# Twelve weight loads of 1 MB each issued as four loads of 256 KB

## The chip, the cores and the metric

The kernel runs on one core of a Trainium2 chip. The metric is the device time of one execution in microseconds (us), as the median of the runs shown. The core has five engines that run beside one another: TensorE (PE, matrix products; its weight loads are listed apart as PEld), VectorE (DVE), ScalarE (ACT), GpSimd (POOL) and SyncE (SP). Each has a queue of instructions of its own and works through it in order. Transfers are issued by SP, ACT or POOL and carried out by the core's 16 DMA engines.

## The reference

One layer of a bidirectional encoder over 1024 tokens (a grid of 16 rows by 64 columns) of width 1024. One projection feeds two groups of heads:

```python
h = _rmsnorm(x, norm_gain[l])
proj = h @ w_in[l]
q_a, k_a, v_a, g_a, q_b, k_b, v_b, g_b = jnp.split(proj, split_at, axis=-1)
...
o_a = _gqa_blocked(q_a, k_a, v_a) * jax.nn.silu(g_a)
o_b = _neighbourhood_attn(q_b..., k_b..., v_b..., na_rpb[l])
o_b = o_b * jax.nn.silu(g_b)
mixed = jnp.concatenate([o_a, o_b], axis=-1)
x = x + mixed @ w_out[l]
return _rmsnorm(x, final_norm_gain)
```

Group A is attention over all 1024 keys (8 query heads, 2 key heads of 64, normalised and rotated by row and column). Group B is attention over a window of 8 rows by 16 columns with a learned bias (8 heads of 64). Everything is float32. The input projection has 3328 columns, the output projection 1024.

## The kernel before

**Weights.** The two weight matrices are cut into 17 groups of 256 columns: `w[0]` to `w[12]` of the input projection and `wo[0]` to `wo[3]` of the output projection (groups 13 to 16). A group is 1024 x 256 float32, 1 MB, and lies in memory as 128 partitions of 8 KB each. It is loaded into a tile `raw` ([128, 8, 256]), of which there are two in turn, so that group g+2 takes the buffer of group g. From `raw` four steps make the operands of the products, a pair of float16 tiles (high and low part): `prep_a` (L281, sum of squares on ACT), `prep_b` (L293 to L295, the sum over partitions on PE, then a power on POOL that gives the scale), `prep_c` (L300, high part on ACT, two halves) and `prep_d` (L307, low part on DVE, two halves). After the last of these the buffer is free, and group g+2 is loaded into it: `load_w`, L159, one DMA issued by POOL. Groups 0 and 1 are loaded at the start by SP, the latter in four pieces of 256 KB (L187).

**Order.** The order of PE is written out by hand for the whole kernel, that of the others only for the opening (up to L875). After it a planner places the instructions of ACT, DVE, POOL and SP on their queues, going by the order in which the program lists them and by its own estimate of when each can run.

The order in which the program lists things comes from a small class, `Flow`. The work is a sequence of slots (`step`). One slot lists, in this order, what is due at "pre", the scores of one attention unit, what is due at "mid", the low part and the transpose of the unit before, what is due at "post", some chunks of the projections (`fill`), and the last products of an older unit. `at(delay, pos, fn)` puts `fn` into the slot that is `delay` slots further on, at the place `pos`. `sums_now` (L341) runs behind a projection chunk and lists `prep_b` of the group that is next, `prep_c` and `prep_d` one slot further on, and `load_w(g + 2)` two slots further on, at "pre" (L349).

**Stages.** In the opening the input is normalised and transposed and the first projections run. Stage A (about 105 to 360 us) has 64 units of the global attention, one head of 128 queries each: scores on PE (L592, L594), their extreme on DVE (L601), two exponentials on ACT (L603 in float16, L604 in float32), the difference of both on DVE (L609), and one DMA transpose of both parts, [128, 2048] float16, issued by SP (L614). Three such tiles are in turn, so ACT's L603 three units later writes where the transpose has read. Four units later PE multiplies the transposed weights by the values (L623 to L625). Between the units run the projections of groups 3 to 8. Stage B (about 360 to 565 us) has 64 units of the neighbourhood attention with smaller scores and transposes (L681 to L705), beside the projections of groups 9 to 12 (the gates) and the output projection; the rest is the output projection of the last rows and the final norm.

Twelve loads are touched by the change, those of groups 5 to 16. Going through the slots, group 5 is loaded at unit 0 of A, 6 at 6, 7 at 14, 8 at 26, 9 at 38, 10 at 50, 11 at 62, then 12 at unit 5 of B, 13 at 15, 14 at 25, 15 at 42 and 16 at 47. Their readers `prep_a` stand at units 10, 22, 34, 46, 58 of A and 2, 11, 21, 37, 43, 49, 54 of B.

Of the kernel before, what the change touches and what calls it, by code (L numbers as in the profile page):

```python
# [42 lines left out]
class Flow:  # L43
# [8 lines left out]
    def at(self, delay, pos, fn, *a):  # L52
        self.due.setdefault((self.slot + delay, pos), []).append((fn, a))
# [35 lines left out]
def kernel(ctx: ExitStack, tc: tile.TileContext, x: bass.AP, w: bass.AP, wo: bass.AP,  # L89
# [3 lines left out]
    act, dve, pool, pe, sp = nc.scalar, nc.vector, nc.gpsimd, nc.tensor, nc.sync  # L93
# [10 lines left out]
    at = fl.at  # L104
# [48 lines left out]
    raw, wp, late, x2 = {}, {}, {}, {}  # L153

    def load_w(g):
        raw[g] = wraw.tile([P, KC, GC], F32, tag="raw", name=f"raw{g}")
        if g in gate:
            pool.tensor_copy(raw[g][:, 0, :1], xr[gate[g]][:, 1:])
        pool.dma_start(raw[g], w[g] if g < 13 else wo[g - 13])  # L159

    xts, gate = [], {}
    ones = area(0, [P], F32)[:1]
# [178 lines left out]
    def sums_now():  # L341

        while pend:
            g = pend.pop(0)
            prep_b(g)
            at(1, "pre", prep_c, g)
            at(1, "post", prep_d, g)
            if g + 2 < 17:
                at(2, "pre", load_w, g + 2)  # L349
# [86 lines left out]
    def qa_gen(hh, up):  # L436
        def evac(pt):
            g = QA + hh
            stg = slot("stg1", [P, 2, 4, P], F16)
            a, b = (0, D) if hh == 0 else (D, 0)  # L440

            def fin(q):
                at(2, "pre", lambda: act.activation(stg[:, :, :, a:a + D], q, AF.Copy))
                at(2, "mid", lambda: dve.tensor_tensor(stg[:, :, :, b:b + D], q, stg[:, :, :, a:a + D], op=OP.subtract))

                def tr():
                    sp.dma_start_transpose(qTa[hh][:, 2 * up:2 * up + 2].rearrange("p i h t -> p (i h) t"),
                                           stg.rearrange("p i a b -> p (i a b)"))
                at(2, "post", tr)
            norm_rope(g, up, pt, 4, 0, fin)  # L450
        yield from proj_pair(QA + hh, up, from_h, evac)

    def kva_gen(up):
        def evac(pt):
            both = slot("stg1", [P, 8, P], F16)
            stg, stg_l = both[:, :6].rearrange("p (i a) b -> p i a b", a=3), both[:, 6:]
            vs = pt[:, :, P:].rearrange("p a (h d) -> p a h d", d=D)
            at(1, "pre", lambda: act.activation(va[:, 2 * up:2 * up + 2, :, 0, :], vs, AF.Copy, scale=2.0 ** -14))

            def vlo():  # L460
                for i in range(2):
                    dve.scalar_tensor_tensor(va[:, 2 * up + i, :, 1, :], vs[:, i], 2.0 ** -14,
                                             va[:, 2 * up + i, :, 0, :], op0=OP.mult, op1=OP.subtract)
            at(1, "mid", vlo)

            def fin(k):
                def hi():
                    act.activation(stg[:, :, :2, :D], k, AF.Copy)
                    act.activation(stg[:, :, :2, D:], k, AF.Copy)
                at(2, "pre", hi)  # L470

                def lo():
                    for h, to in ((0, stg[:, :, 2]), (1, stg_l)):
                        dve.tensor_tensor(to.rearrange("p i (e d) -> p i e d", d=D),
                                          k[:, :, h, None, :].to_broadcast([P, 2, 2, D]),
                                          stg[:, :, h].rearrange("p i (e d) -> p i e d", d=D), op=OP.subtract)
                at(2, "mid", lo)

                def tr():
                    sp.dma_start_transpose(kTa[:, 2 * up:2 * up + 2].rearrange("p i a t -> p (i a) t"),  # L480
                                           both[:, :6].rearrange("p a b -> p (a b)"))
                    sp.dma_start_transpose(klo1[:, 2 * up:2 * up + 2], stg_l.rearrange("p a b -> p (a b)"))
                at(2, "post", tr)
            norm_rope(KVA, up, pt[:, :, :P], 2, 1, fin)
        yield from proj_pair(KVA, up, from_h, evac)
# [92 lines left out]
    def group(g, gens):  # L578

        def first(gen):  # L580
            prep(g + 1)
            yield from gen
        return [first(gens[0]) if g < 16 else gens[0], *gens[1:]]
# [255 lines left out]
    k, q = [kva_gen(up) for up in UP], group(1, [qa_gen(0, up) for up in UP])  # L839
# [30 lines left out]
    x_rs(7)  # L870
    x_y(7)
    load_w(2)
    gate[3] = 5
    x_lo(7, dve)
    load_w(3)  # L875

    for p in range(11):
# [165 lines left out]
```

## Time and profile before

| | |
|---|---|
| runs | 611.54, 610.44, 607.44 us; median 610.44 us |
| the profiled execution | 611.81 us, of which the span in the trace is 610.0 us |
| granted clock of TensorE, mean | 0.967 |
| busy: PE, DVE, ACT, POOL | 88%, 72%, 65%, 20% of the span |
| transfers issued by POOL | 19.92 MB in 3312 packets, 11.6% of the DMA engines' time |
| transfers issued by SP | 75.66 MB in 242306 packets, 67.7% |
| the weight loads of L159 | 15, median time from issue to landing 6.7 us (groups of `w`), 5.9 us (`wo`) |

The loads of groups 5 to 16 are issued at 101.92, 129.72, 160.71, 205.59, 252.25, 303.04 and 348.76 us, and in stage B at 381.51, 408.73, 438.29, 485.97 and 505.71 us.

A row of a timeline gives the start, the duration, the engine, the line, the operation and its operands, and in brackets how long the engine stood idle before it and what ended that. A row of a group gives the least, median and largest duration in nanoseconds. For a DMA issue the duration is the time that the issuing queue needed, not the time of the transfer; that is "to landing". A busy share of DMA engines near 1 means that packets were in work on them all the time, whatever they moved.

### The profile page before, as it was taken

The page shows a single profiled execution, that of the slowest core. Times are in us where ns is not written, and L with a number is a line of the kernel's source. Part 1 is how long each engine was busy: PE and PEld are TensorE (multiplying, and loading weights), DVE is VectorE, ACT ScalarE, POOL GpSimd, SP SyncE. Part 2 cuts the span into 40 slices and gives each one's busy share as a digit, 9 for nine tenths or more (in the row PEclk, how much of TensorE's full clock was granted, in tenths as well). Part 3 has the DMA queues.
Part 4 walks back from the last instruction along what each step waited for, and adds up shares of the span by engine and source line. Part 5 has one row for each costly group of instructions (what it writes and reads, how often), then busy time and mean ns, then how long its engine had stood idle before and what let it go on. Part 6 is the DMA issues. An engine that isn't in the chain of part 4 may idle for free.

```text
span 610.0 us, 13863 instructions
## 1 busy us (share of the span) xinstructions
PE 534.4 (88%) x5541; PEld 405.4 (66%) x5541; DVE 440.6 (72%) x986; ACT 394.9 (65%) x647; POOL 119.3 (20%) x150
## 2 busy tenths in 40 slices
PE   3587989799988979979888979999999789889794
PEld 1376878577864535547666767877777567668684
DVE  4688676987977948957977847586877866778332
ACT  5552454878859858858667727677689986674210
POOL 2396788410000000000000000110111221112100
PEclk9978999999999979989899999999999898999899
DMA  8989433799999999999799894548486996687422
GB/s 231 225 160 247 96 105 106 136 213 195 204 198 168 197 173 169 206 207 187 155 183 210 155 217 122 118 76 134 103 149 122 172 212 145 134 140 183 95 62 70
DMA packets 245972, 97.26 MB, mean 159 GB/s; under 512 B 236561, under 2 KB 237201, under 8 KB 243986
## 3 DMA queue, kind: packets, MB, share of 16 engines
q1 hardware_dynamic: 242306, 75.66, 67.7%
q0 software_dynamic: 3312, 19.92, 11.6%
q10 hardware_dynamic: 288, 0.79, 0.5%
q8 instruction: 43, 0.70, 0.5%
q14 instruction: 23, 0.19, 0.1%
HBM read 31.33 MB, written 4.19 MB: 58 GB/s over the span
## 4 chain that ended last, share of the span: by engine, by line
PE 44%; DMA 14%; issue 14%; DVE 13%; POOL 6%; ACT 5%; SPq 1%; DVEq 0%; POOLq 0%; ACTq 0%
PE pj L369 14%; PE wt L369 7%; DMA ar<-p 6%; PE po L369 5%; PE kb L369 4%; DMA ar<-ar 4%; PE s L592 3%; PE s L594 2%; POOL nt L417 2%; PE sb L674 2%; DVE whl L307 2%; ACT p L604 2%; DVE p L601 1%; PE sb L673 1%; ACT p L603 1%
## 5 line engine op out<-in xcount | busy, mean ns | idle before, releaser
L369 PEld LDWEIGHTS <-hT 128*128 128x128 f16 x2112 | 205.6, 100 | 68.5 <-issue 15.4
L369 PE MATMUL pj<-whl,hT 128*128 128x256 f16 x1584 | 189.2, 275 | 3.4 <-DMA hT<-xhl 1.8
L601 DVE CUSTOM_DVE_ANT_0 p<-s,sm 128x1024 f32<-128x1024 f32 x64 | 82.0, 1281 | 15.4 <-PE s L594 13.9
L603 ACT ACTIVATE p<-s,nm,sm 128x1024 f16<-128x1024 f32 x43 | 51.8, 1204 | 51.1 <-DMA ar<-p 23.4
L369 PE MATMUL wt<-whl,hT 128*128 128x256 f16 x528 | 68.0, 286 | 14.9 <-ACT whl L300 7.1
L604 ACT ACTIVATE p<-s,nm,sm 128x1024 f32<-128x1024 f32 x64 | 76.8, 1200 | 0.0
L609 DVE TENSOR_TENSOR p<-p,p 128x1024 f16<-128x1024 f32 x43 | 52.8, 1229 | 21.7 <-ACT p L604 21.6
L369 PE MATMUL po<-whl,mA 128*128 128x256 f16 x384 | 65.8, 277 | 0.0
L684 ACT ACTIVATE rq<-ar,mx,sm 128x384 f32<-128x384 f32 (+1 forms) x64 | 43.0, 673 | 28.6 <-DVE mx L683 28.4
L295 POOL TENSOR_TENSOR sm<-wss,mh 128x1 f32<-128x1 f32 x17 | 11.0, 645 | 250.1 <-DVE wss L294 237.4
L369 PEld LDWEIGHTS <-mA 128*128 128x128 f16 x512 | 48.7, 100 | 12.3 <-issue 5.0
L369 PE MATMUL po<-whl,mB 128*128 128x256 f16 x192 | 53.1, 277 | 0.0
L592 PE MATMUL s<-kTa,rq 128*128 128x512 f16 x128 | 39.5, 391 | 14.6 <-ACT p L604 14.6
L623 PE MATMUL pv<-va,ar 128*128 128x64 f16 x384 | 39.3, 194 | 8.7 <-DMA ar<-p 7.4
L307 DVE SCALAR_TENSOR_TENSOR whl<-raw,sm,whl 128x1024 f16<-128x1024 f32 (+1 forms) x33 | 44.8, 1371 | 1.9 <-ACT whl L300 1.9
L685 ACT ACTIVATE ar<-ar,mx,sm 128x384 f16<-128x384 f32 (+1 forms) x64 | 42.9, 674 | 1.1
L623 PEld LDWEIGHTS <-ar 128*128 128x128 f16 x384 | 34.7, 99 | 13.1 <-DMA ar<-p 9.3
L300 ACT ACTIVATE whl<-raw,sm 128x1024 f16<-128x1024 f32 x34 | 37.1, 1138 | 5.0 <-POOL sm L295 4.9
L681 DVE CUSTOM_DVE_ANT_0 ar<-sb,bias 128x384 f32<-128x384 f32 x48 | 26.6, 555 | 18.4 <-PE sb L674 15.4
L625 PE MATMUL pv<-va,ar 128*128 128x64 f16 x384 | 39.3, 194 | 0.0
L624 PE MATMUL pv<-va,ar 128*128 128x64 f16 x384 | 39.3, 194 | 0.0
L690 DVE TENSOR_TENSOR ar<-rq,ar 128x384 f16<-128x384 f32 (+1 forms) x64 | 34.1, 533 | 4.8 <-ACT ar L685 4.8
(196 smaller groups left out, 1069.3 us busy)
## 6 DMA issues: line engine op xcount, KB each, us to landing
raw<-in_w_dram POOLq DMA_DIRECT2D x11, 1024.0 KB, 6.7
raw<-in_wo_dram POOLq DMA_DIRECT2D x4, 1024.0 KB, 5.9
x<-in_x_dram SPq DMA_DIRECT2D x7, 512.0 KB, 6.4
khh<-ar SPq DMA_DIRECT2D x16, 128.0 KB, 3.7
x2b<-in_x_dram POOLq DMA_DIRECT2D x4, 512.0 KB, 5.9
x<-in_x_dram POOLq DMA_DIRECT2D x4, 512.0 KB, 6.8
out_dram<-x2b SPq DMA_DIRECT2D x8, 256.0 KB, 3.0
out_dram<-x SPq DMA_DIRECT2D x7, 256.0 KB, 2.9
```

The costliest lines, as they stand in the source:

```text
L307: dve.scalar_tensor_tensor(wp[g][1][:, s], raw[g][:, s], col(S_ + g), wp[g][0][:, s], op0=OP.mult, op1=OP.subtract)
L369: pe.matmul(*o[0], **o[1])
L592: pe.matmul(s[:, c * 512:(c + 1) * 512], q, kTa[:, 4 * c:4 * c + 4, hh], start=True, stop=False)
L601: dve.tensor_tensor_reduce(out=p32, in0=s, in1=col(SHA).to_broadcast([P, 1024]), scale=col(NSA), scalar=3e38, op0=OP.add, op1=OP.min, accu ...
L603: act.activation(hl[:, 0], s, AF.Exp, bias=nm, scale=col(SCA))
L604: act.activation(p32, s, AF.Exp, bias=nm, scale=col(SCA), accum_out=sums[hh, u][:, h:h + 1])
L609: dve.tensor_tensor(hl[:, 1], p32, hl[:, 0], op=OP.subtract)
L623: pe.matmul(o, pt[:, kt], va[:, kt, hh, 0], start=kt == 0, stop=False)
L624: pe.matmul(o, pt[:, kt], va[:, kt, hh, 1], start=False, stop=False)
L625: pe.matmul(o, pt[:, 8 + kt], va[:, kt, hh, 0], start=False, stop=kt == 7)
L684: act.activation(p32, t, AF.Exp, bias=mx, scale=col(SCB + hh), accum_out=sums["b", u][:, h:h + 1])
L685: act.activation(hl[:, 0], t, AF.Exp, bias=mx, scale=col(SCB + hh))
```

## The change

A load of groups 5 to 16 becomes four loads, each of two of the eight 256-column rows that a partition holds (2 KB per partition, 256 KB in all). The first is listed where the whole load stood, the others one, two and three slots later, at "pre". Groups 2 to 4 are loaded as before.

```diff
         if g in gate:
             pool.tensor_copy(raw[g][:, 0, :1], xr[gate[g]][:, 1:])
-        pool.dma_start(raw[g], w[g] if g < 13 else wo[g - 13])
+        src = w[g] if g < 13 else wo[g - 13]
+        if g < 5:
+            pool.dma_start(raw[g], src)
+            return
+        for i in range(4):
+            k = slice(2 * i, 2 * i + 2)
+            issue = lambda k=k: pool.dma_start(raw[g][:, k], src[:, k])
+            at(i, "pre", issue) if i else issue()
```

## The prediction

> **What bounds the kernel now.** I read the page first (busy shares, slices), then the busy time by windows, then the queue of SyncE beside the weight loads, then who waited for whom, and last GpSimd's timeline, since that engine issues the loads. The first fence has rows of the windows: stretch, then busy time of PE, PEld, DVE, ACT, POOL, then granted clock, DMA share, GB/s.
>
> ```profile
> 105.00:366.00 261.00, 232.38 (x2723) 163.44 (x2721) 206.23 (x344) 187.10 (x250) 16.02 (x20) 0.97 1.00 188
> 400.00:450.00 50.00, 50.00 (x527) 39.85 (x525) 37.56 (x112) 37.38 (x72) 6.53 (x10) 1.00 0.64 117
> ```
>
> The first is the global attention (stage A), the second lies in the neighbourhood attention (stage B). In A the PE is idle 28.6 of 261 us while the DMA engines are booked all the time; in B the PE does not stop. So a change in how weights come in can earn something in A alone. What the DMA engines carry there is one 128x2048 transpose per attention unit, issued by SyncE at L614. These are its issues beside the six loads that start in A; the first line is the usual time of one.
>
> ```profile
> L614 SPq DMA_TRANSPOSE ar<-p x32: 1467/2150/6552, 111.4 to 350.8; - x32
> 131.83 5.85 SPq L614 DMA_TRANSPOSE ar<-ar  x1
> 159.18 9.00 SPq L614 DMA_TRANSPOSE ar<-p  x2
> 207.95 5.80 SPq L614 DMA_TRANSPOSE ar<-p  x1
> 254.92 6.42 SPq L614 DMA_TRANSPOSE ar<-p  x1
> 299.09 9.97 SPq L614 DMA_TRANSPOSE ar<-p  x2
> 350.84 6.55 SPq L614 DMA_TRANSPOSE ar<-p  x1
> ```
>
> An issue that takes 2.15 us by itself takes 5.8 to 6.55 us beside a load: about 4 us more, each time. ACT then waits, since the transpose still reads the tile that ACT writes next (L603):
>
> ```profile
> ACT p L603 <- DMA ar<-p: 23.4, 9, 4.7
> 217.36 1.21 ACT L603 ACTIVATE p<-s,nm,sm 128x1024 f16<-128x1024 f32 x1 [4.73 <-DMA ar<-p]
> 263.48 1.21 ACT L603 ACTIVATE p<-s,nm,sm 128x1024 f16<-128x1024 f32 x1 [3.78 <-DMA ar<-p]
> 312.48 1.21 ACT L603 ACTIVATE p<-s,nm,sm 128x1024 f16<-128x1024 f32 x1 [4.30 <-DMA ar<-p]
> ```
>
> And PE waits for ACT. The idle stretches of PE behind the six loads, the first, the last and the sum of the six, and two stretches in which the clock came back late:
>
> ```profile
> 144.00:150.00 6.00, 5.05 (x60) 4.09 (x58) 3.59 (x6) 5.06 (x9) 0.00 (x0) 1.00 0.97 196
> 357.00:366.00 9.00, 5.61 (x99) 4.78 (x97) 2.85 (x6) 0.31 (x1) 0.00 (x0) 1.00 1.02 162
> sum 42.00, PE 25.57 PEld 19.17 DVE 18.00 ACT 20.08 POOL 0.00; mean PE 4.26 PEld 3.19 DVE 3.00 ACT 3.35 POOL 0.00
> 217.00:226.00 9.00, 7.15 (x63) 3.55 (x64) 3.65 (x4) 7.07 (x9) 0.00 (x0) 0.62 0.96 187
> 266.00:269.00 3.00, 3.00 (x8) 1.05 (x8) 2.31 (x2) 2.21 (x3) 0.00 (x0) 0.50 1.12 212
> ```
>
> 42.0 - 25.6 = 16.4 us of idle PE, and 7.15 x 0.38 + 3.00 x 0.50 = 4.2 us of slow clock. So 20.6 us is the most that gentler loads could earn, an upper bound, because part of it belongs to other copies in the same stretches.
>
> **The change part by part.** Twelve loads (groups 5 to 16) become 48: piece 0 where the load stood, pieces 1 to 3 put into the flow one, two and three slots later.
>
> *When the pieces go out.* The text says successive slots. A slot of A holds one attention unit, and each unit has one DVE pass over its scores:
>
> ```profile
> L601 DVE CUSTOM_DVE_ANT_0 p<-s,sm x64: 1272/1283/1285, 105.9 to 351.4; 128x1024 f32<-128x1024 f32 x64
> ```
>
> So a slot is about (351.4 - 105.9) / 63 = 3.9 us. But a slot is a place in the order in which instructions are written; only PE's order is kept by hand there, and an engine runs on unless an instruction waits. So what counts is what lies between the pieces on GpSimd's queue, and what they wait for.
>
> ```profile
> 199.99 0.56 POOL L295 TENSOR_TENSOR sm<-wss,mh 128x1 f32<-128x1 f32 x1 [38.71 <-DVE wss L294]
> 205.59 0.57 POOL L159 DMA_DIRECT2D raw<-in_w_dram  x1 [5.04 <-DVE whl L307]
> 246.12 0.56 POOL L295 TENSOR_TENSOR sm<-wss,mh 128x1 f32<-128x1 f32 x1 [39.96 <-DVE wss L294]
> 523.32 1.12 POOL L763 DMA_DIRECT2D x<-in_x_dram  x2 [6.81 <-DVE whl L307]
> ```
>
> After the load at 205.59 GpSimd does nothing for 40 us. The load waits for the last read of its buffer (DVE, L307); a later piece waits for the same read, which is then past, and for nothing else. The last row is the precedent: two loads into two halves of one tile, the second right behind the first, 1.12 us for both. So I expect the pieces of A at distances of about 0.57 us, all four out within 4 x 0.57 = 2.3 us, not over three slots (11.7 us). What changes in A is then the piece and not the time: rows of 2 KB per partition in place of 8 KB, 256 KB at a time.
>
> *What that does to the transposes.* The bytes are the same. No trace shows four pieces beside a transpose of A. The nearest rows are in stage B: transposes beside no load, beside one load of 1 MB (408.7), and beside two of 512 KB with 4 KB rows (the row at 523.32). Issues, then time to landing as least, median and most:
>
> ```profile
> L692 SPq DMA_TRANSPOSE ar<-ar x3: 1212/1227/1642, 398.3 to 401.6; - x3
> DMA to landing us min/median/max: 2.8/3.2/4.4
> L692 SPq DMA_TRANSPOSE ar<-ar x4: 1212/1844/2123, 409.0 to 415.0; - x4
> DMA to landing us min/median/max: 4.3/5.7/6.6
> L692 SPq DMA_TRANSPOSE ar<-ar x4: 1211/1660/2906, 523.6 to 528.5; - x4
> DMA to landing us min/median/max: 4.9/7.2/8.1
> ```
>
> Halves are no gentler than the whole: 7.2 against 5.7 us, some of it because those transposes stand closer together. So the bounds for A are a gain of all 20.6 us and a loss of 7.2 - 5.7 = 1.5 us for each of the six loads, 9 us. I take 0: the row nearest to four pieces in 2.3 us is the one of two pieces in 1.1 us, it shows no relief, and what it shows as a loss is mixed with crowding.
>
> The Trainium skill ("DMA: Bandwidth & Descriptors", Queues, rings and completion order) says that a DMA engine takes turns between queues and hands over only at the end of a packet. By it smaller pieces would give the transposes more turns within one load, and the sum would be lower by the second rival below; the rows of halves do not bear that out.
>
> *GpSimd's own time.* 36 further issues of 0.57 us are 20.5 us of GpSimd, which is busy 16.0 of the 261 us of A (first fence). In A and most of B they fall into its idle time (the 40 us above). Where it matters is the load of group 5, in the last of the rotary work, which is a chain between GpSimd and DVE:
>
> ```profile
> 101.92 0.64 POOL L159 DMA_DIRECT2D raw<-in_w_dram  x1
> 103.59 1.66 POOL L417 TENSOR_TENSOR nt<-nt,mh 128x8 f32<-128x8 f32 x1 [1.04 <-DVE nt L416]
> 106.12 1.41 POOL L425 TENSOR_TENSOR ar<-ar,tabs 128x256 f32<-128x256 f32 x2 [0.87 <-DVE ar L421]
> 108.52 1.27 POOL L429 TENSOR_TENSOR ar<-ar 128x512 f32<-128x512 f32 x1 [0.99 <-DVE nt L416]
> ```
>
> Three issues (1.7 us) against gaps of 1.04, 0.87 and 0.99 us: nothing if one falls into each gap, 3 x 0.57 - 1.04 = 0.7 us if all stand before the work at 103.59, 1.7 us if none finds a gap. I take 0.6.
>
> *The reader.* ACT's square of a group (L281) now waits for four landings. In A it stands 10 to 20 slots behind the load (load 8 in unit 26, its reader in unit 46). The two last groups have no such room:
>
> ```profile
> 485.97 0.56 POOL L159 DMA_DIRECT2D raw<-in_wo_dram  x1 [3.19 <-DVE whl L307]
> 492.01 1.89 ACT L281 ACTIVATE whl<-raw 128x2048 bf16<-128x2048 f32 x1
> 505.71 0.63 POOL L159 DMA_DIRECT2D raw<-in_wo_dram  x1 [5.25 <-DVE mx L683]
> 510.94 0.72 POOL L715 TENSOR_TENSOR mB<-mB,ar 128x256 f32<-128x256 f32 x1 [4.60 <-DVE ar L713]
> 511.72 1.91 ACT L281 ACTIVATE whl<-raw 128x2048 bf16<-128x2048 f32 x1 [0.90 <-DMA raw<-in_wo_dram]
> ```
>
> Group 16 is waited for already (0.90 us) and 15 is read 6.0 us after its issue. With the last piece 1.7 us later each wait grows by up to 1.7 us; ACT is in order, and the exponentials of B stand behind. Ends: 0 (the reader is ordered later) and 3.4 us; a piece queued behind the product at 510.94 would cost 4.6 us more. I take 1.2, since PE has other work in part of that time.
>
> *Sum.* 0 + 0.6 + 1.2 = 1.8 us. The profiled execution took 611.81 us (span 610.0 and 1.8 around it), so 613.6 on its own time; it was 1.4 us above the median of 610.44, so the prediction on the median is 612.2, in round numbers **612**. Own range of this case: 0 to +6 and 2 us of spread between runs, 608 to 617.
>
> **The rivals.**
> 1. *The slots do space the pieces* (a wait per piece that I do not see). Then a transpose meets a quarter of a load: some 4 / 4 = 1 us more on 2.15, 3.15 us in a slot of 3.9. The stalls would go but for the other copies; two thirds of 20.6 us, 14 us: 597. For it: the size of the stalls. Against it: the 40 idle microseconds and the row at 523.32. Chance 0.10.
> 2. *Smaller packets let the transposes through*, though all four pieces go out at once. If the load is drawn over two transposes in place of one, each is 2 us late instead of 4, about half of the stalls goes, 10 us: 602. For it: the load has no hurry in A, the transposes have. Against it: the rows of halves. The skill's rule named above is this one. Chance 0.17.
> 3. *The pieces hold the transposes longer* (slower). Place: L614 behind each load in A. Price: by the halves 1.5 us for each of six loads, 9 us: 620. It decides from 1 us per load on, since 6 us is 1%. For it: the third pair of landings. Against it: ACT has some slack before a late transpose stops it. Chance 0.17.
>
> **How the numbers follow.** The forecast has 0.56, the rivals 0.10, 0.17 and 0.17. About 1% (6.1 us: below 604.3, above 616.5) is what a measurement of this kernel can tell from no change. Faster by more: 0.10 + 0.15 of rival 2 = 0.25. Slower by more: 0.14 of rival 3 and 0.04 of the forecast = 0.18. Within: 0.57. The range is 602 to 618: it leaves out rival 1 and the upper part of rival 3, together under 0.2.
>
> **What would show it.** Right: after a load of A, four issues on GpSimd 0.6 us apart; transposes of 5 to 7 us on SyncE behind them; ACT's wait for `ar<-p` near 23 us; L281 of groups 15 and 16 waiting 1 to 3 us. Wrong: pieces 3 to 4 us apart (rival 1); transposes near 3 us beside pieces that leave together, and PE's idle time in A well under 28.6 us (rival 2); transposes above 7 us and more idle PE (rival 3). An order of ACT, DVE or SyncE that came out otherwise for the same work would spoil the comparison by some microseconds either way.

## The result, and the profile after

The changed kernel took 626.28 us (median of four runs, 624.17 to 632.54) beside 610.99 us of the kernel before on the same chip. The ratio is 1.028, with a 95% interval of 1.022 to 1.034: slower. The profiled execution took 625.74 us with a span of 624.0 us and a mean granted clock of 0.950 (before: 611.81, 610.0 and 0.967). Medians and ratios here and below are of executions in the faster of two states; one execution, of spaced_by_partition at 626.73 us, was in the slower.

The first view of the changed kernel is GpSimd's timeline at two of the loads (in this kernel L159 has become L165, and every later line is seven further on).

```profile
210.02 2.17 POOL L165 DMA_DIRECT2D raw<-in_w_dram  x4 [5.05 <-DVE whl L314]
307.86 2.17 POOL L165 DMA_DIRECT2D raw<-in_w_dram  x4 [6.86 <-DVE whl L314]
```

All four pieces are out within 2.2 us, in one row: the slots did not space them. The next lines are SyncE's timeline of before behind group 10's load, then SyncE's and ACT's timelines of the changed kernel behind it (the second of the two loads above), and the line of the waits that answers to `ACT p L603` of before.

```profile
309.16 3.74 SPq L614 DMA_TRANSPOSE ar<-ar  x1
```

```profile
304.03 8.43 SPq L621 DMA_TRANSPOSE ar<-p  x2
312.56 8.96 SPq L621 DMA_TRANSPOSE ar<-ar  x1
322.09 1.21 ACT L610 ACTIVATE p<-s,nm,sm 128x1024 f16<-128x1024 f32 x1 [9.10 <-DMA ar<-p]
```

```profile
ACT p L610 <- DMA ar<-p: 26.0, 7, 9.1
```

The transpose behind group 10's load holds the queue for 9.0 us, where the row that stands in its place before has 3.7, and ACT waits 9.1 us in one piece, where it waited 4.3. The sum of these waits grew little (23.4 to 26.0 us); one of them doubled. Two windows show what it does to PE, first of the kernel before and then of the changed one (stretch, busy time of PE, PEld, DVE, ACT and POOL, granted clock, DMA share, GB/s). Each begins 2 us after the issue of group 10's load and holds the whole of ACT's long wait behind it.

```profile
305.00:325.00 20.00, 17.20 (x238) 13.56 (x235) 15.24 (x24) 13.24 (x18) 0.00 (x0) 1.00 1.07 188
```

```profile
310.00:330.00 20.00, 13.44 (x135) 9.54 (x134) 10.22 (x17) 9.79 (x13) 0.03 (x1) 0.74 1.08 150
```

PE stands idle for 6.6 us in place of 2.8, and its granted clock is 0.74 in place of 1.00. The DMA engines are booked above 1 in both and move less in the changed kernel, 150 GB/s in place of 188. The page's queue lines say the same of the whole span: as many bytes as before, a larger share of time.

```profile
q1 hardware_dynamic: 242306, 75.66, 69.0%
q0 software_dynamic: 5424, 19.93, 13.0%
```

Along the span the lag is spread. GpSimd's powers of the weight scales (L295 before, L302 after) are a mark that both kernels pass once per group: it is 1.6 us late at 124 us, 3.1 at 155, 3.5 at 246, 5.2 at 295, 8.1 at 343 (behind group 10), 10.3 at 479 and 14.7 at the last one. Group 10 is therefore one place of several.

A second thing changed that the diff does not show. The planner put ACT, DVE, POOL and SP in another order: in the opening of stage A on all four queues, and in the last quarter mainly on DVE and ACT. By the two lists of the queues that the experiments use, 58 of DVE's 856 places and 19 of ACT's 464 hold another instruction. The sum of squares of group 16, for one, is now read at 529.47 us with no wait (511.72 with 0.90 before).

### The profile page after: what moved, and what is told of

Same layout as the page of the kernel before. It is cut to its first block, busy times and chain, and to the rows that moved or that the text cites. A ratio compares the mean times of both kernels' runs of the same rounds, so it can differ in the third digit from the quotient of the medians.

```text
span 624.0 us, 13943 instructions
## 1 busy us (share of the span) xinstructions
PE 540.2 (87%) x5541; PEld 408.5 (65%) x5541; DVE 443.3 (71%) x986; ACT 394.6 (63%) x647; POOL 138.6 (22%) x186
## 4 chain that ended last, share of the span: by engine, by line
PE 30%; DMA 20%; issue 18%; DVE 12%; ACT 9%; POOL 8%; SPq 2%; DVEq 0%; POOLq 0%; ACTq 0%
PE pj L376 10%; DMA ar<-p 9%; PE wt L376 4%; PE po L376 4%; DMA ar<-ar 3%; PE kb L376 3%; DMA mB<-mhl 2%; DMA x2b<-in_x_dram 2%; ACT p L611 2%; DVE whl L314 2%; POOL nt L424 1%; PE s L599 1%; POOL ar L432 1%; ACT p L610 1%; ACT whl L288 1%
## 5 line engine op out<-in xcount | busy, mean ns | idle before, releaser
L376 PE MATMUL pj<-whl,hT 128*128 128x256 f16 x1584 | 193.0, 279 | 6.5 <-DVE ar L509 2.7
L376 PE MATMUL wt<-whl,hT 128*128 128x256 f16 x528 | 67.6, 285 | 14.7 <-ACT whl L307 7.1
L616 DVE TENSOR_TENSOR p<-p,p 128x1024 f16<-128x1024 f32 x43 | 54.3, 1262 | 25.6 <-ACT p L611 25.5
L302 POOL TENSOR_TENSOR sm<-wss,mh 128x1 f32<-128x1 f32 x17 | 10.9, 639 | 255.9 <-DVE wss L301 243.2
L376 PE MATMUL po<-whl,mA 128*128 128x256 f16 x384 | 64.2, 273 | 0.0
L630 PE MATMUL pv<-va,ar 128*128 128x64 f16 x384 | 40.0, 196 | 11.8 <-DMA ar<-p 11.8
L314 DVE SCALAR_TENSOR_TENSOR whl<-raw,sm,whl 128x1024 f16<-128x1024 f32 (+1 forms) x33 | 44.8, 1371 | 4.4 <-ACT whl L307 4.4
L631 PE MATMUL pv<-va,ar 128*128 128x64 f16 x384 | 40.0, 196 | 0.0
L632 PE MATMUL pv<-va,ar 128*128 128x64 f16 x384 | 40.0, 195 | 0.0
L688 DVE CUSTOM_DVE_ANT_0 ar<-sb,bias 128x384 f32<-128x384 f32 x48 | 26.6, 555 | 17.6 <-PE sb L681 13.3
```

The costliest lines, as they stand in the source:

```text
L314: dve.scalar_tensor_tensor(wp[g][1][:, s], raw[g][:, s], col(S_ + g), wp[g][0][:, s], op0=OP.mult, op1=OP.subtract)
L376: pe.matmul(*o[0], **o[1])
L616: dve.tensor_tensor(hl[:, 1], p32, hl[:, 0], op=OP.subtract)
L630: pe.matmul(o, pt[:, kt], va[:, kt, hh, 0], start=kt == 0, stop=False)
L631: pe.matmul(o, pt[:, kt], va[:, kt, hh, 1], start=False, stop=False)
L632: pe.matmul(o, pt[:, 8 + kt], va[:, kt, hh, 0], start=False, stop=kt == 7)
```

## The experiments

To tell the loads from the order, the queue order of one kernel is held by hand in another: behind the last slot, every instruction of ACT, DVE, POOL and SP that belongs to the planned part gets an edge to its predecessor in the wanted list. The edge orders the two on one queue and adds no semaphore.

```diff
+    for engine, key in ((act, "Activation"), (dve, "DVE"), (pool, "Pool"), (sp, "SP")):
+        ...
+        line = [i for k in queue_order(key) for i in groups[k]]
+        ...
+        for a, b in zip(line, line[1:]):
+            if b.name not in opening:
+                tc.add_manual_dep(b, a.name, later, reason="order")
```

The pieces 1 to 3 of a load stand right behind piece 0 in that list, unless the text says otherwise. All ratios are to the kernel before on the same chip, whose medians in the four groups of runs were 608.55, 608.42, 609.83 and 609.25 us; a ratio on record is not the quotient of the two medians and can differ from it (by up to 0.3%, and by 0.5% for spaced_by_partition, which has three runs). In the cuts of code below, `...` stands for lines left out.

| run | loads | order | median us | ratio, 95% interval |
|---|---|---|---|---|
| pieces_old_order | all 12 in pieces | before | 620.64 | 1.0189 (1.0129 to 1.0248) |
| whole_new_order | whole | changed | 615.90 | 1.0112 (1.0078 to 1.0147) |
| pieces_A_old_order | 6 to 11 in pieces | before | 615.20 | 1.0084 (1.0050 to 1.0117) |
| spaced_A_old_order | 6 to 11 in pieces, spaced | before | 610.56 | 1.0026 (0.9994 to 1.0058) |
| four_by_partition | all 12, cut by partitions | before | 627.02 | 1.0281 (1.0232 to 1.0329) |
| pieces_but_10 | all but 10 in pieces | before | 612.81 | 1.0051 (1.0017 to 1.0084) |
| pieces_B_old_order | 12 to 16 in pieces | before | 612.77 | 1.0062 (1.0031 to 1.0092) |
| spaced_by_partition | 6 to 11, by partitions, spaced | before | 618.46 | 1.0114 (1.0045 to 1.0184) |
| only_group_10 | 10 in pieces | before | 614.18 | 1.0079 (1.0043 to 1.0115) |
| only_group_9 | 9 in pieces | before | 608.57 | 0.9958 (0.9930 to 0.9987) |
| late_group_10 | 10 in pieces, held back | before | 608.28 | 0.9979 (0.9949 to 1.0008) |
| halves_old_order | all 12 in halves | before | 608.90 | 0.9983 (0.9950 to 1.0015) |
| change_but_10 | all but 10 in pieces | changed | 617.77 | 1.0137 (1.0071 to 1.0204) |
| change_late_10 | all in pieces, 10 held back | changed | 618.41 | 1.0153 (1.0085 to 1.0221) |
| all_pieces_late_10 | all in pieces, 10 held back | before | 613.57 | 1.0063 (1.0026 to 1.0100) |

### The pieces or the order

```diff
-        pool.dma_start(raw[g], w[g] if g < 13 else wo[g - 13])
+        src = w[g] if g < 13 else wo[g - 13]
+        if not (g >= 5):      # in pieces_A_old_order: not (6 <= g < 12)
+            pool.dma_start(raw[g], src)
+            return
+        for i in range(4):
+            k = slice(2 * i, 2 * i + 2)
+            ins = pool.dma_start(raw[g][:, k], src[:, k])
+            ...
```

whole_new_order is the kernel before with its one load per group and the changed kernel's list of the queues.

Expected of pieces_old_order:

> All twelve loads in four pieces, issued one behind the other; the queues of ACT, DVE, POOL and SP otherwise held in the order that they have in the kernel before. Theory P (the pieces themselves cost, by holding the transposes): 620 to 628 us, as the changed kernel. Theory O (the planner's other order costs, the pieces are harmless): 609 to 613 us. If each has a share: in between, and the distance from 611 is the share of the pieces.

Expected of whole_new_order:

> Whole loads of 1 MB as in the kernel before, with the queues of ACT, DVE, POOL and SP held in the order of the changed kernel. Theory P: 609 to 613 us. Theory O: 620 to 628 us. Both theories together with the run of the pieces in the old order must add up to the 14 us of the change, unless the two act on each other.

Expected of pieces_A_old_order:

> Old order held; only the loads of groups 6 to 11 (stage A) in four pieces, one behind the other. Theory P: slower than before by about 1 us for each of the six loads, 615 to 620 us, seen as longer transposes at L614 behind the loads. Theory O: 609 to 613 us.

Both parts cost: 1.9% for the pieces in the order of before and 1.1% for the order alone. Their sum, 3.0%, is the change's 2.8% within the intervals. In whole_new_order part of the price shows in the opening, on GpSimd's timeline (the answering rows of before stand in the prediction, from 103.59 us on):

```profile
103.51 1.66 POOL L480 TENSOR_TENSOR nt<-nt,mh 128x8 f32<-128x8 f32 x1 [1.04 <-DVE nt L479]
105.56 2.01 POOL L480 TENSOR_TENSOR nt<-nt,mh 128x8 f32<-128x8 f32 x1 [0.39 <-DVE nt L479]
107.54 1.85 POOL L488 TENSOR_TENSOR ar<-ar,tabs 128x256 f32<-128x256 f32 x2
157.03 0.57 POOL L358 TENSOR_TENSOR sm<-wss,mh 128x1 f32<-128x1 f32 x1 [25.81 <-DVE wss L357]
```

The second power of the rotary part (L480) goes ahead of the first product (L488), which before came in between; the mark of the next group stands at 157.03 in place of 155.31 us, 1.7 us late. By the spans of the two profiled executions (612.9 and 610.0 us) the order costs 2.9 us, by the medians 7.4; where the rest lies was not found.

Behind group 10's load pieces_old_order has the long transpose and the long wait of the change; these are its SyncE and ACT timelines:

```profile
298.85 9.70 SPq L685 DMA_TRANSPOSE ar<-p  x2
308.65 9.19 SPq L685 DMA_TRANSPOSE ar<-ar  x1
318.41 1.20 ACT L674 ACTIVATE p<-s,nm,sm 128x1024 f16<-128x1024 f32 x1 [10.48 <-DMA ar<-p]
```

### Pieces that are really spaced

Here piece 1, 2 and 3 each wait for a softmax sum of a later attention unit: a copy of one of its columns into the piece's place goes first on GpSimd.

```diff
+        def issue(i):
+            k = slice(2 * i, 2 * i + 2)
+            late[first, i] = [pool.tensor_copy(raw[g][:, 2 * i, :1], late["sum"]).ins.name,
+                              pool.dma_start(raw[g][:, k], src[:, k]).ins.name]
+            ...
+        for i in range(1, 4):
+            at(1 * i, "pre", issue, i)
```

Expected of spaced_A_old_order:

> Old order held; the loads of groups 6 to 11 in four pieces, and here each later piece really waits: GpSimd first copies one column of the softmax sum of the attention unit of that slot into the piece's place, so the pieces leave one unit (about 3.9 us) apart. My first rival of the prediction: if spacing is what the transposes need, 597 to 606 us, with no transpose issue of L614 above 4 us behind these loads. If the total of transfers in stage A is the limit and not their bunching: 609 to 613 us. The pieces of POOL stand 3 to 4.5 us apart either way.

GpSimd's timeline shows that the spacing took place, and the waits and the window of stage A what it brought:

```profile
206.47 0.58 POOL L226 DMA_DIRECT2D raw<-in_w_dram  x1 [5.05 <-DVE whl L382]
210.34 0.54 POOL L231 DMA_DIRECT2D raw<-in_w_dram  x1 [0.30 <-POOL raw L230]
213.46 0.54 POOL L231 DMA_DIRECT2D raw<-in_w_dram  x1 [0.30 <-POOL raw L230]
220.65 0.54 POOL L231 DMA_DIRECT2D raw<-in_w_dram  x1 [0.30 <-POOL raw L230]
```

```profile
ACT p L678 <- DMA ar<-p: 20.0, 8, 5.1
ACT ar L678 <- DMA ar<-ar: 6.6, 6, 3.0
```

```profile
105.00:366.00 261.00, 232.59 (x2713) 163.92 (x2711) 207.00 (x346) 188.72 (x250) 35.10 (x55) 0.97 1.04 187
```

The pieces of this load lie 3 to 7 us apart (over the six loads 1.0 to 8.6), and the stage is what it was: PE is busy for 232.59 us (232.38 before), and these two waits of ACT for transposes come to 26.6 us (20.0 + 6.6; before 23.4 and 4.5). They are about as many (14, before 13) and the longest is no shorter (5.1 us, before 4.7). The same bytes pass, and the DMA share of the stage is 1.04 (1.00 before).

### Rows of 8 KB

Four issues again, but each of 32 partitions with their whole rows, so that the rows are as long as before.

```diff
+            k = slice(32 * i, 32 * i + 32)
+            ins = pool.dma_start(raw[g][k], src[k])
+            ...
```

Expected of four_by_partition:

> Old order held; all twelve loads in four issues again, but cut by partitions: each moves 32 partitions with their whole 8 KB rows, so the number of issues and GpSimd's time are those of the pieces and the rows are those of the whole load. If the short rows (2 KB, four times as many packets) are the cost: 606 to 611 us, and packets of the POOL queue as many as before. If the number of issues, their waits or GpSimd's time are the cost: 617 to 623 us, as the pieces in the old order.

Expected of spaced_by_partition:

> As the spaced pieces of groups 6 to 11, one attention unit apart, but cut by partitions with whole 8 KB rows; the rest of the loads whole, old order held. The spaced pieces with 2 KB rows gave the time of before. If their spacing earned something that the short rows took back: 598 to 606 us. If bunching costs nothing that spacing can earn: 607 to 612 us.

They cost as much as pieces of short rows or more, 2.8% unspaced (627.02 us, above the 617 to 623 expected) and 1.1% spaced. So it is not the length of the rows that makes a load in four parts dear. Why the spaced ones lose 1.1% where those of columns lose 0.3% stays open; the two intervals just overlap.

### Which load

```diff
-        if not (g >= 5):
+        if not (g >= 5 and g != 10):    # pieces_but_10
+        if not (g > 11):                # pieces_B_old_order
+        if not (g == 10):               # only_group_10; g == 9 in only_group_9
```

Expected of pieces_but_10:

> Old order held; all loads in four pieces by rows as in the changed kernel, but that of group 10 whole. In all three profiles with pieces the load of group 10 (near 300 us) is the one place of stage A where ACT waits 9 to 11 us for a transpose instead of 4.3. If that place is the cost in A: 5 us less than all in pieces, 613 to 617 us. If the cost is spread over all loads of A: 619 to 622 us.

Expected of pieces_B_old_order:

> Old order held; only the loads of groups 12 to 16 (stage B) in four pieces. My prediction's term for the readers of groups 15 and 16 was 1.2 us, at most 3.4 us. If it holds: 609 to 612 us. If stage B has the other half of the cost of the pieces (12 us for all, 6.6 us for groups 6 to 11): 613 to 616 us, with ACT's square of groups 15 and 16, or what stands behind it, later than before.

Expected of only_group_10:

> Group 10's load alone in four pieces, every queue otherwise in the order of before. If this one load costs by itself what separates all pieces from all but group 10 (620.6 - 612.8 = 7.8 us), the ratio to before is 1.010 to 1.016, its last piece lands some 12 us after its issue, and ACT's wait for ar<-p behind it is about 10 us in place of 4.3. If it takes the other pieces too (the lag that groups 5 to 9 in pieces leave brings load 10 to another moment), the ratio is within 1.004 and the wait under 6 us.

Expected of only_group_9:

> Group 9's load alone in four pieces, order of before: the control to only_group_10. A load of stage A in pieces that costs by the mean of groups 6 to 9 and 11 is 1.004 at most; if any load in pieces costs what group 10's does, 1.010 or more.

Leaving one load of twelve whole takes the price from 1.9 to 0.5%; that one load alone in pieces costs 0.8%, below the range expected of it, and group 9's alone nothing (its gain of 0.4% is less than the 1% that the prediction takes as the least that can be told from no change). What is left with group 10 whole, 0.5%, is as much as the loads of stage B cost by themselves, 0.6%; both are below that 1%, too. ACT's readers of groups 15 and 16 wait longer, here in ACT's timeline of pieces_B_old_order:

```profile
495.22 1.91 ACT L352 ACTIVATE whl<-raw 128x2048 bf16<-128x2048 f32 x1 [3.89 <-DMA raw<-in_wo_dram]
517.96 1.91 ACT L352 ACTIVATE whl<-raw 128x2048 bf16<-128x2048 f32 x1 [6.86 <-DMA raw<-in_wo_dram]
```

Before, the same two waited 0 and 0.90 us. In pieces_but_10 it is 2.37 and 2.95 us. That these waits are the price of stage B is likely but not shown: halves_old_order (below) has waits of 4.8 us there in all and no price.

### The moment

In late_group_10 the four pieces of group 10 go out back to back as in only_group_10, but behind a copy that waits for a softmax sum of the next unit.

```diff
+        def issue():
+            first = pool.tensor_copy(raw[g][:, 0, :1], late["sum"]).ins.name
+            for i in range(4):
+                ...
+        at(1, "pre", issue)      # g == 10 alone
```

Expected of late_group_10:

> Group 10's load alone in four pieces, all four back to back but one attention unit later (a copy of one column of a softmax sum goes first on GpSimd and holds them back), the order of before otherwise. If what costs is the moment at which the pieces meet the transposes, one unit's shift changes it: ratio within 1.004, no wait of ACT for ar<-p above 6 us. If group 10 in pieces costs whenever it goes out, the ratio stays where only_group_10 has it.

The pieces left 1.3 us later, and the price was gone: 0.998 in place of 1.008. The DMA view of 298 to 318 us shows what changed. Each pair of fences has the load's issue by GpSimd with two issues of transposes by SyncE, then what was moved in each half microsecond, and packets, MB and share of time by queue (q0 carries the load, q1 the transposes). First only_group_10:

```profile
302.51 2.18 POOL L228 DMA_DIRECT2D raw<-in_w_dram  x4 [6.95 <-DVE whl L378]
303.42 3.64 SPq L685 DMA_TRANSPOSE ar<-p  x1
307.16 10.27 SPq L685 DMA_TRANSPOSE ar<-ar  x1
```

```profile
GB/s 208 9 0 85 213 215 217 204 115 0 0 66 221 246 229 164 209 203 223 164 55 112 37 41 86 70 209 107 105 65 134 129 52 122 102 101 89 66 32 236
q1 hardware_dynamic: 5584, 1.41, 65.7%
q0 software_dynamic: 320, 1.05, 30.8%
```

And late_group_10:

```profile
303.85 2.19 POOL L231 DMA_DIRECT2D raw<-in_w_dram  x4 [0.30 <-POOL raw L228]
303.28 3.46 SPq L689 DMA_TRANSPOSE ar<-p  x1
306.84 5.19 SPq L689 DMA_TRANSPOSE ar<-ar  x1
```

```profile
GB/s 11 0 0 146 214 215 218 204 53 0 0 0 6 193 93 0 5 10 258 289 375 173 303 393 393 372 265 244 279 290 288 249 217 220 212 149 0 78 209 211
q1 hardware_dynamic: 9326, 2.35, 71.8%
q0 software_dynamic: 320, 1.05, 16.2%
```

In both the DMA engines have nothing to do when the load is issued (the zeros near 303 us). In the first the pieces go out 0.9 us before SyncE's transpose and their packets come first; from 308 us on packets of both are in work side by side, and together they move about 100 GB/s. In the second they go out 0.6 us behind that transpose, and the packets of transposes come first; transposes move at 290 GB/s, the load by itself at up to 390, one after the other, and the load is through by 312 us. A packet of the load was in work for 30.8% of 16 x 20 us / 320 = 0.31 us in the first and 0.16 us in the second, one of a transpose for 38 and 25 ns. Over the ten microseconds from 308 to 318 us the same view gives for only_group_10

```profile
DMA packets 2546, 0.98 MB, mean 98 GB/s; under 512 B 2458, under 2 KB 2458, under 8 KB 2546
```

and for late_group_10

```profile
DMA packets 5930, 2.46 MB, mean 246 GB/s; under 512 B 5674, under 2 KB 5674, under 8 KB 5930
```

The windows of 305 to 325 us show what that is worth to PE, first in only_group_10, then in late_group_10: PE is busy for 11.95 us at a granted clock of 0.74 in the one, and for 17.11 us at 1.00 in the other.

```profile
305.00:325.00 20.00, 11.95 (x121) 8.60 (x118) 9.87 (x17) 8.81 (x12) 0.00 (x0) 0.74 1.06 140
305.00:325.00 20.00, 17.11 (x221) 13.31 (x220) 15.07 (x26) 13.73 (x18) 1.04 (x2) 1.00 1.09 202
```

The whole load of the kernel before also goes out 0.9 us ahead of the transpose, on idle engines, but is nearly through when the transpose's packets start:

```profile
GB/s 219 110 0 0 78 214 213 220 201 124 0 0 131 229 147 246 360 328 344 193 227 114 240 8 8 84 292 281 292 289 290 122 108 212 216 218 204 91 33 214
```

The other five loads of stage A leave while a transpose's packets are in work (217 to 250 GB/s in the half microsecond from the issue on in pieces_old_order, 103 to 222 in the changed kernel); group 10 is the one of the six that finds zeros in both. Zeros alone do not make a load dear: late_group_10 finds them too, and so do four of the five loads of pieces_B_old_order, which cost 0.6% together. Where group 10's pieces are dear they go out ahead of a 128x2048 transpose, by 0.9 us in pieces_old_order and in the changed kernel as well. No other lead was tried, so how long before the transpose they would do no harm is not known. halves_old_order changes the number of pieces to two of 512 KB, in the same code.

Expected of halves_old_order:

> All twelve loads in two pieces of 512 KB (4 KB rows), order of before. If the cost comes with the number of issues (12 further ones in place of 36), it is a third of that of quarters: ratio near 1.006. If any cut at all brings it, near 1.019. If halves are as gentle as a whole load, within 1.003.

Two pieces are free, though group 10's two also go out 0.9 us ahead of the transpose on idle engines: the issues of the transposes there take 5.2 and 3.8 us, as before (5.1 and 3.7). So it takes four issues and that moment together. The two traces differ in when the transpose's first packets come: with four pieces at about 305.8 us, 2.4 us after its issue and with some 0.6 MB of the load still to come, with two at about 307.6 us, 4.4 us after its issue and with the load nearly through. Why four parts let them in so early, and why both then crawl, was not settled.

### The moment in the change itself

The same two edits, a whole load of group 10 and a later one, in the changed kernel's own order, and the later one with all pieces in the order of before:

Expected of change_but_10:

> The change with its own order of the queues (held by hand) and all its pieces, but group 10's load whole. If the pieces cost through the one moment at group 10 and the order costs apart from that, what is left is the order's 1.011 and 1.005 of the other pieces: 1.013 to 1.018, and ACT's longest wait for ar<-p is under 6 us. If another load takes over as the one that goes badly, or the cost in the change is spread over all loads, it stays at 1.022 or more.

Expected of change_late_10:

> As change_but_10, but group 10 too in four pieces, all four back to back and held one attention unit by a copy that waits for a softmax sum. If only the moment counts: the same ratio as change_but_10, 1.013 to 1.018, with a transpose's packets in work on the DMA engines when the pieces begin. If group 10's pieces cost by being pieces: 1.022 or more.

Expected of all_pieces_late_10:

> All twelve loads in four pieces, order of before, group 10's four held one attention unit. Pieces in the order of before cost 1.019 with group 10 at its place and 1.005 with group 10 whole. If the moment is what counts: 1.000 to 1.008. If group 10's pieces cost by being pieces: 1.015 or more.

All three came out where the moment puts them: 1.014, 1.015 and 1.006. In change_late_10 the pieces leave 1.6 us behind the transpose, with its packets in work (210 GB/s); in all_pieces_late_10 0.6 us behind it, on idle engines, as in late_group_10. In change_but_10 the wait behind group 10 is back at its old length on ACT's timeline:

```profile
316.15 1.20 ACT L676 ACTIVATE p<-s,nm,sm 128x1024 f16<-128x1024 f32 x1 [4.31 <-DMA ar<-p]
```

The marks on GpSimd place it: between the powers that frame group 10's load (295.27 and 342.68 us before, 47.4 us) 50.4 to 52.2 us pass where its four pieces go out at once at their place (the change, pieces_old_order, pieces_A_old_order, four_by_partition, only_group_10), 48.6 and 49.4 us where they are spaced, and 44.8 to 47.6 us where they are held back, halved or whole, in the order of before or in the changed one.

So the change's 2.8% consist of about 1.1% for the order (whole_new_order), 1.4% for group 10's moment (1.028 less 1.014; in the order of before 1.019 less 1.005) and 0.3% for the other eleven loads (1.014 less 1.011; in the order of before 0.5%). By the intervals a difference of two ratios is uncertain by 0.7 to 0.9 points, so the first two are clear of zero and the third is not. That group 10's pieces cost 1.4% in company and 0.8% alone lies within this uncertainty. No kernel here is faster than the one before by 1%.

## Why the prediction was wrong

The forecast was 612.2 us with 608 to 617 as its own range, and 618 as the upper end; the time was 626.28.

*When the pieces go out*: right. Four issues in one row of 2.17 us, 0.54 us each, where 0.57 was said.

*GpSimd's own time in the opening*, +0.6 us: of the right size. In pieces_old_order the load of group 5 goes out 0.28 us earlier than before (101.64 us) and GpSimd's next work starts 0.29 us later (103.88), so the three issues put in 0.57 us there.

*What that does to the transposes*, taken as 0 between -20.6 and +9: the first step that failed. For five of the six loads 0 is what the runs show (pieces_but_10 costs no more than pieces_B_old_order, and only_group_9 nothing). The bound of 9 us was nearly reached by one load alone: 1.4% of 610 us is 8.5 us, in one place (52.2 us between the two marks in pieces_old_order, 44.8 in pieces_but_10, are 7.5). The reasoning spread the loss evenly, 1.5 us for each of six, from rows of stage B in which loads and transposes stood differently to each other. Nor was it looked at, load by load, what SyncE issues just behind a load. The row of 9.97 us is two issues with a gap between them: 1.84 us from 299.09 us on and, 0.9 us behind group 10's load, 5.11 us from 303.94 us on. (So not every issue beside a load takes 5.8 us or more.) The third rival named the right sign, line and sum of this part (9 us), but not one load at one moment.

*The reader*, +1.2 us between 0 and 3.4: mis-sized, as far as the runs show, for the order of before. The waits of groups 15 and 16 grew from 0.9 to 5.3 us (pieces_but_10) and to 10.8 us (pieces_B_old_order), since the last piece came later than the 1.7 us of three issues: in pieces_B_old_order group 16 is read 517.96 - 506.71 = 11.3 us after its first issue, before it was 511.72 - 505.71 = 6.0 us. The price of the loads of stage B is 0.5 to 0.6%, 3 to 4 us; that the readers' waits are all of it is not shown, since halves_old_order has 4.8 us of them and loses nothing. In the changed kernel itself the planner had moved the readers, and they wait 0.7 us in all.

*What was not in the sum*: the planner's order. The last lines of the prediction said that another order would spoil the comparison by some microseconds either way, and no term, no chance and no end of the range came of it. It cost 1.1%, 7 us (whole_new_order), with every load whole. A sum of the terms as measured, 0.6 + 8.5 + 3 + 7, is some 19 us, against 15 that the change cost; the readers' share is smaller in the new order, and the rest lies within the intervals.

*The first rival* is refuted twice. The slots do not space the pieces, and where they are spaced (spaced_A_old_order) it brings nothing: +0.3%, between -0.1 and +0.6, in place of the 14 us that the rival offered. The upper bound of 20.6 us was idle time that lies behind loads; spread over the stage the loads left as much of it (PE busy for 232.59 us, before 232.38). That the bytes moved away from one transpose meet the next is the likely reason and was not shown.

*The second rival*, transposes let through by smaller packets, has its counterpart in the rows above: packets of both queues are in work in the same microseconds for 10 us behind group 10's load. The Trainium skill ("DMA: Bandwidth & Descriptors", Queues, rings and completion order) describes turns between queues at the ends of packets. The trace agrees so far as that packets of both queues pass in every microsecond from 308 to 317 us; it shows 100 GB/s for both together where they ran one after the other at 290 to 390. The transpose was later for it, not earlier: the one issued at 303.42 us in only_group_10 landed 14.6 us after its issue, the one in its place before (303.94 us) after 8.5 us.

## What to carry to other kernels

A slot in the program is a place in an order, and where a planner makes the queues, an edit of the issues can move instructions that it does not name; hold the order of one kernel in the other before a difference is put down to the edit. Before loads are split or spaced, look, load by load, at what the other queues issue just before and behind each one: half of the price here came from one of twelve, whose four pieces went out 0.9 us ahead of a transpose, and 0.6 us behind it that part was gone. In this stage, with the DMA engines booked all the time, spreading the same bytes gained nothing (1.003).

## What the runs showed of the hardware that was not expected

A load in four issues and the 128x2048 transposes, with packets of both in work at once, moved 98 GB/s for 10 us (only_group_10, 308 to 318 us), while the same transfers 1.3 us later went one after the other at 290 and up to 390 GB/s. The DMA share is near 1 in both, so it does not tell them apart (88 and 30% for the two queues in the first, 70 and 32% in the second over those 10 us); the GB/s do. That a load is issued on idle DMA engines does not decide it, since both were. Four issues of 32 partitions with rows of 8 KB were no gentler than four with rows of 2 KB (1.028 and 1.019), and two issues of 512 KB cost nothing (0.998).
